# A chain of attention, cross-attention and 32 routed experts: down projection as three products of 12-bit halves, norm weights moved to the gathered rows, splits of 1024 columns

## The chip, the cores and the metric

The kernel runs on one core of one Trainium2 chip. The metric is the device time of one execution in microseconds (us). A core has a matrix engine (TensorE, PE in the profile; its weight loads are PEld), three engines for elementwise work (VectorE or DVE, ScalarE or ACT, GpSimd or POOL), and SyncE (SP), which here issues DMAs. Each engine runs its own instructions strictly in the order in which they stand in its queue; semaphores order them between engines.

## The reference, cut to what matters

A decoder layer on 1024 rows of 1024 columns: attention and retention (not touched here), a cross-attention, then a mixture of 32 experts, of which each row is sent to two.

```python
def rms_norm(x, g):
    y = xf * lax.rsqrt(jnp.mean(xf * xf, axis=-1, keepdims=True) + EPS)
    return (y * g).astype(x.dtype)
...
    x = x + memory_cross_attention(...)                       # "x2" in the kernel
    hm = rms_norm(x, moe_norm_g[l])
    x = x + hierarchical_moe(hm, ...)
...
        a = jnp.einsum('sd,edf->sef', hr, w_gate)             # 1024 -> 256, each expert
        u = jnp.einsum('sd,edf->sef', hr, w_up)
        act = jax.nn.silu(a) * u * gate[:, :, None]
        return jnp.einsum('sef,efd->sd', act, w_down)         # 256 -> 1024
```

All is float32. The kernel computes an expert only for the rows sent to it, in lists of 96 rows (`CAP`).

## The kernel before, in words

Most matrix products are made as three products of halves. A number x is split into H, x rounded to a 12-bit mantissa (type `F32R`, a copy on ACT), and L = x - H (on DVE); then `mm3` (L145) adds up H*H, H*L and L*H in PSUM. `split` (L151) makes the halves; with a `scale` it multiplies on the way (L157 on ACT, L158 on DVE), without one it is L154 and L155.

The last two stages matter here.

- *End of the cross-attention* (763 to 862 us of the profiled execution). For each of eight tiles of 128 rows, `column` (L1077) makes x2 (L1087 adds the residual), sums squares, and when a tile is whole SP writes it to DRAM twice (L1091): to `x2d`, from which the experts gather rows, and to `out`, into which the experts add. Tiles are transposed for the router's logits. Then the reciprocal norm `rx` (a power on POOL, L168) and the lists of rows are made (862 to 881).
- *The experts* (881 to 1226), `moe` (L1478). Expert e's weights come by `load_up` (gate and up, 1 MB each) and `load_down` (1 MB), issued on SP into rings of five raw buffers each; up to five experts are loaded ahead. A list's rows are gathered from `x2d` by POOL's indirect DMA (L1411) into `xg`, transposed by PE and split into xH and xL (`expert_x`, two blocks b0, b1). `expert_up` splits the gate and up weights with the norm's weights `g8` as the scale, one 128x512 slice n at a time, in four pairs j0 to j3 (`half` 0 and 1), and `mm3` adds them up in one PSUM tile `ps_pj`. `expert_act`: silu on ACT (`sl`, L1448), product on DVE (`act`, L1450). `expert_actT`: two PE transposes (L1456), a copy on ACT (`aT`, L1459). `expert_out`: the down product in full f32, straight from the raw weights (L1469, `ps_sc`), scaled by the gate into `y` (one half on ACT, L1473, one on DVE, L1471), and added into `out` by POOL's indirect DMA, the scatter (L1474). Scatters into rows of the same group wait for each other.

The loop makes, for expert e, its act, the first half of the up projection of e+1, the transposed act of e, the gathered rows of e+2, the down projection of e, and the second half of the up projection of e+1. A scheduler then orders each engine's queue by a table of priorities (not changed) and by the free buffers of the tiles: `H` and `L` have HB buffers, the gathered rows NX, `y` YB. The chip runs that order; it doesn't depend on what is late at run time.

## Time and profile before

| | us |
|---|---|
| three runs | 1228.27, 1231.3, 1240.53 (median 1231.3) |
| the profiled execution: time | 1227.24 |
| its span, from the first to the last instruction | 1225.4 |
| PE busy | 1160.0 (95%) |
| DVE busy | 791.2 (65%) |
| ACT busy | 657.4 (54%) |
| POOL busy | 154.8 (13%) |
| mean granted TensorE clock (1 is 2.4 GHz) | 0.986 |

The profile is one execution, seen on each engine. PE's share over the whole is high, but a share over the whole mixes stages; what a change to the experts is worth is read from their stage alone, 881 us to the end, which is 28% of the span. By lines, the splits of the expert weights (L158 on DVE, L157 on ACT) and the products (L145, L1469 on PE) are its largest groups. The page's chain of work that ended last gives PE 64% and DMA 19% of the span.

### The profile page before, as it was taken

How to read it: one execution, taken by the hardware profiler on the slowest of the kernel's cores; microseconds unless marked ns; L12 is line 12 of the kernel's file. 1: busy time of each engine (PE TensorE's matmuls, PEld its weight loads, DVE VectorE, ACT ScalarE, POOL GpSimd, SP SyncE). 2: the span in 40 equal slices, each digit the busy share in tenths (PEclk: the TensorE clock that was granted, in tenths of full speed). 3: DMA queues.
4: the chain of work that ended last, by engine and by line, in shares of the span. 5: the costliest groups of instructions: out<-in, count | busy, mean ns of one | idle time of the engine just before them, and what ended most of it. 6: DMA issues, size and time to landing. Idle time of an engine off the chain costs nothing.

```text
span 1225.4 us, 18474 instructions
## 1 busy us (share of the span) xinstructions
PE 1160.0 (95%) x6309; PEld 907.3 (74%) x6309; DVE 791.2 (65%) x2056; ACT 657.4 (54%) x1540; POOL 154.8 (13%) x151
## 2 busy tenths in 40 slices
PE   7999999998799999989999999999699999999994
PEld 6887878776588778878899998778566666666552
DVE  4756465678777877557744445554677777777571
ACT  8723232456455565557644445332477777777571
POOL 1011010121000000000000000000222222222121
PEclk9999999999999999999999999999799999999997
DMA  7622020204223424266621025975799999999972
GB/s 227 180 65 80 10 76 10 89 23 149 87 73 112 147 78 121 86 221 202 221 71 61 27 62 159 329 273 223 239 347 341 334 337 332 321 312 319 316 271 32
DMA packets 115362, 213.25 MB, mean 174 GB/s; under 512 B 20531, under 2 KB 68659, under 8 KB 107073
## 3 DMA queue, kind: packets, MB, share of 16 engines
q1 hardware_dynamic: 108096, 194.66, 46.8%
q0 software_dynamic: 7168, 17.37, 6.1%
q8 instruction: 51, 0.84, 0.3%
q14 instruction: 47, 0.38, 0.1%
HBM read 179.69 MB, written 40.11 MB: 179 GB/s over the span
## 4 chain that ended last, share of the span: by engine, by line
PE 64%; DMA 19%; DVE 6%; ACT 5%; issue 3%; POOL 1%; SPq 0%; POOLq 0%; DVEq 0%; ACTq 0%
PE ps_pj L145 36%; DMA raw<-in_expert_w_up_dram 5%; DMA raw<-in_expert_w_down_dram 5%; PE ps_fl L145 5%; PE ps_sc L1469 4%; PE ps_sc L145 4%; PE ps_po L145 4%; PE ps_tr L162 3%; DMA raw<-in_expert_w_gate_dram 3%; DMA raw<-in_cross_w_kv_dram 2%; DVE wl L158 1%; PE ps_tr L1422 1%; PE ps_pjp L145 1%; DMA raw<-in_cross_w_q_dram 1%; ACT wh L157 1%
## 5 line engine op out<-in xcount | busy, mean ns | idle before, releaser
L145 PE MATMUL ps_pj<-wh,xT 128*128 128x512 f32 (+1 forms) x640 | 218.1, 401 | 1.9 <-ACT wh L157 1.8
L158 DVE SCALAR_TENSOR_TENSOR L<-raw,g,H 128x512 fp32r<-128x512 f32 x256 | 179.9, 746 | 58.4 <-ACT H L157 57.0
L157 ACT ACTIVATE H<-raw,g 128x512 fp32r<-128x512 f32 x256 | 169.4, 713 | 34.7 <-PE ps_pj L145 22.6
L145 PEld LDWEIGHTS ps_pj<-wh,xT 128*128 128x128 f32 x640 | 120.1, 189 | 21.0 <-ACT wh L157 2.7
L145 PE MATMUL ps_pj<-wl,xT 128*128 128x512 f32 (+1 forms) x320 | 126.3, 395 | 0.0
L1469 PE MATMUL ps_sc<-raw,aT 128*96 128x512 f32 x256 | 117.6, 602 | 1.0 <-ACT aT L1459 1.0
L145 PE MATMUL ps_pj<-H,xH 128*96 128x512 f32 x256 | 116.3, 454 | 0.3 <-ACT H L157 0.3
L145 PE MATMUL ps_pj<-L,xH 128*96 128x512 f32 x256 | 102.8, 401 | 0.6 <-DVE L L158 0.6
L145 PE MATMUL ps_pj<-H,xL 128*96 128x512 f32 x256 | 101.5, 397 | 0.0
L1469 PEld LDWEIGHTS ps_sc<-raw,aT 128*96 128x96 f32 x256 | 39.1, 162 | 64.9 <-issue 51.1
L1474 POOL DMA_INDIRECT out_dram<-y,idx x32 | 59.6, 1863 | 208.8 <-ACT H L157 163.2
L145 PE MATMUL ps_pj<-x1TH,wh 128*128 128x256 f32 x256 | 74.3, 290 | 2.3 <-ACT x1TH L154 2.3
L145 PE MATMUL ps_pj<-x1TL,wh 128*128 128x256 f32 x256 | 75.3, 294 | 0.0
L145 PE MATMUL ps_pj<-x1TH,wl 128*128 128x256 f32 x256 | 74.4, 291 | 0.0
L145 PEld LDWEIGHTS ps_pj<-wl,xT 128*128 128x128 f32 x320 | 60.7, 190 | 8.0
L145 PEld LDWEIGHTS ps_pj<-H,xH 128*96 128x96 f32 x256 | 42.5, 166 | 23.5 <-issue 7.2
L145 PEld LDWEIGHTS ps_pj<-L,xH 128*96 128x96 f32 x256 | 41.6, 163 | 22.9 <-DVE L L158 9.1
L453 ACT ACTIVATE tg<-ps_pj,rh 128x128 f32<-128x128 f32 x32 | 11.7, 365 | 84.9 <-PE ps_pj L145 84.7
L145 PEld LDWEIGHTS ps_pj<-H,xL 128*96 128x96 f32 x256 | 41.4, 162 | 15.4 <-issue 0.3
L145 PEld LDWEIGHTS ps_pj<-x1TH,wh 128*128 128x128 f32 x256 | 48.5, 189 | 2.7 <-ACT x1TH L154 2.7
L1023 ACT ACTIVATE cP<-ps_sc,cnb,fcq 128x256 f32<-128x256 f32 x32 | 17.8, 558 | 58.5 <-DVE cnb L1018 58.5
L145 PEld LDWEIGHTS ps_pj<-x1TH,wl 128*128 128x128 f32 x256 | 48.6, 190 | 0.0
(410 smaller groups left out, 2898.1 us busy)
## 6 DMA issues: line engine op xcount, KB each, us to landing
raw<-in_expert_w_down_dram SPq DMA_DIRECT2D x32, 1024.0 KB
raw<-in_expert_w_gate_dram SPq DMA_DIRECT2D x32, 1024.0 KB
raw<-in_expert_w_up_dram SPq DMA_DIRECT2D x32, 1024.0 KB
raw<-in_w_in_dram SPq DMA_DIRECT2D x32, 256.0 KB
raw<-in_cross_w_kv_dram SPq DMA_DIRECT2D x32, 256.0 KB
x<-x1d SPq DMA_DIRECT2D x16, 512.0 KB
xr<-in_x_dram SPq DMA_DIRECT2D x16, 256.0 KB
raw<-in_w_out_dram SPq DMA_DIRECT2D x16, 256.0 KB
```

What stands on the lines that cost most here:

```text
L145: mm = lambda s, m, i, e: self.nc.tensor.matmul(out, s, m, start=i, stop=e, skip_group_check=skip)
L157: self.high = nc.scalar.activation(H, src, AF.Copy, scale=scale)
L158: return nc.vector.scalar_tensor_tensor(L, src, scale, H.bitcast(F32), OP.mult, OP.subtract)
L162: self.nc.tensor.transpose(dst[:, i * 128:(i + 1) * 128], src[:, i * 128:(i + 1) * 128], self.ident)
L453: nc.scalar.activation(tg, p[:, 384:512], AF.Tanh, scale=rh[:, tb:tb + 1])
L1023: nc.scalar.activation(P[:, js], s[:, js], AF.Exp, bias=nb[:, j:j + 1], scale=f[:, j:j + 1], accum_out=su[:, j:j + 1])
L1422: nc.tensor.transpose(tr[:, k * CAP:(k + 1) * CAP], xg[:CAP, 4 * b + k::8], self.ident[:CAP, :CAP])
L1469: nc.tensor.matmul(py[:CAP], act[:, j * CAP:(j + 1) * CAP], wd[:, j, cs], start=(j == 0), stop=(j == 1))
L1474: return nc.gpsimd.indirect_dma_start(out=self.out, out_offset=bass.IndirectOffsetOnAxis(ap=rows, axis=0), in_=y[:CAP], in_offset=None, co ...
```

## The change

The down projection's weights and the transposed activation are now split, and the product is made by `mm3` (three f32r products for each f32 one). The norm's weights `g8` are no longer multiplied into the expert weights; instead a copy `gx` of the norm's weights on all partitions is multiplied into x2 before it is written to `x2d`: on POOL a whole tile at a time (`gained`), in the last tile in pieces, one on POOL and two on DVE. Splits of the expert weights have 128x1024 elements instead of 128x512 (six per expert on each of ACT and DVE, four for gate and up and two for down, where it was eight), so HB goes from 6 to 4; NX goes from 4 to 3 and YB from 4 to 2. Both halves of `y` are written by ACT. The down weights are laid out as the others are, two neighbouring rows on a partition, and the activation is transposed with a stride of 2 to match. In the diff, the new places are L1095 and L1100 (multiply), L1400 (load), L1436 (transposes of rows), L1455 (`expert_split`), L1462 and L1464 (`sl`, `act`), L1470 (transposes of act) and L1485 (`y`).

```diff
--- before.py
+++ after.py
@@ -50,8 +50,8 @@
 ND = 5
 RING = {"gu": (0, 4, 4, 5), "dn": (1, 1, 5, 5)}
 LOADS = ["u0", "u1", "", "u2", "", "u3", "d1", "d2d3d4"]
-NX = 4
-YB = 4
+NX = 3
+YB = 2
 HP = 1
 XB = 4
 WK = 2
@@ -69,7 +69,7 @@
 ES = 1
 SP = 0
 OB = 2
-HB = 6
+HB = 4
 HALVES = [(slice(0, 64), slice(64, 128)), (slice(64, 128), slice(0, 64))]
 TWO_PI = 2.0 * math.pi
 C1 = 6.28125
@@ -151,7 +151,7 @@
 
         nc = self.nc
         if scale is None:
-            nc.scalar.activation(H, src, AF.Copy)
+            self.high = nc.scalar.activation(H, src, AF.Copy)
             return nc.vector.tensor_tensor(L, src, H.bitcast(F32), OP.subtract)
         else:
             self.high = nc.scalar.activation(H, src, AF.Copy, scale=scale)
@@ -1052,7 +1052,7 @@
         s2 = self.s2
         self.s2l = sm.tile([128, 1], F32, name="s2l", bufs=1)
         self.r2 = sm.tile([128, NT], F32, name="rx2", bufs=1)
-        x2s, ocs, oTs, pls, hs, ps = {}, {}, {}, {}, {}, {}
+        x2s, ocs, oTs, pls, hs, ps, gs = {}, {}, {}, {}, {}, {}, {}
 
         def load_oc(tb):
             if tb < NT:
@@ -1087,8 +1087,18 @@
             nc.vector.tensor_tensor(x2[:, cols], p, x2[:, cols], OP.add)
             self.square(self.s2l if q.start else s2[:, tb, c:c + 1], x2[:, cols], p)
             if cols.stop == D:
-                for dst in (self.x2d, self.out):
-                    nc.sync.dma_start(dst[tb * 128:(tb + 1) * 128, :], x2)
+                nc.sync.dma_start(self.out[tb * 128:(tb + 1) * 128, :], x2)
+            if tb == NT - 1:
+                if q.start == 0:
+                    gs[c] = self.slot([128, 512], name="ocl", bufs=OB, pool=self.OT)
+                g = gs[c][:, q]
+                (nc.vector if c else nc.gpsimd).tensor_tensor(g, x2[:, cols], self.gx[:, cols], OP.mult)
+                nc.sync.dma_start(self.x2d[tb * 128:(tb + 1) * 128, cols], g)
+
+        def gained(tb):
+
+            nc.gpsimd.tensor_tensor(x2s[tb], x2s[tb], self.gx, OP.mult)
+            nc.sync.dma_start(self.x2d[tb * 128:(tb + 1) * 128, :], x2s[tb])
 
         def transposed(tb, i, n=4):
 
@@ -1181,11 +1191,15 @@
                         column(tb, 1, slice(0, 8), slice(0, 256))
                         logits(j, 0)
                         transposed(tb - 1, 1)
+                        gained(tb - 1)
                         column(tb, 1, slice(0, 4), slice(256, 512))
                         transposed(tb, 1, 2)
                     with self.at("fl1", j):
                         logits(j, 1)
                     end(j)
+                    if tb + 1 < NT:
+                        gained(tb - 1)
+                        gained(tb)
                 with self.at("fbeg", tb):
                     begin(tb + 2)
                 load_oc(tb + 3)
@@ -1199,8 +1213,8 @@
 
         nc, a, G = self.nc, self.a, self.G
         one = lambda shape, name, dtype=F32, pool=G: pool.tile(shape, dtype, name=name, bufs=1)
-        self.g8 = one([128, 8], "g8")
-        nc.sync.dma_start(self.g8, a["moe_norm_g"][0].rearrange("(p k) -> p k", k=8))
+        self.gx = one([128, D], "gx", pool=self.P)
+        nc.sync.dma_start(self.gx, a["moe_norm_g"][0].partition_broadcast(128))
         self.wr = one([128, 8, 36], "wr", pool=self.P)
         gm = one([128, 8], "gm", pool=self.P)
         nc.sync.dma_start(gm, a["moe_norm_g"][0].rearrange("(k p) -> p k", p=128))
@@ -1383,7 +1397,7 @@
         w = self.a[("expert_w_gate", "expert_w_up", "expert_w_down")[i]][0]
         w = w[e] if isinstance(e, int) else w[bass.ds(e, 1)].rearrange("o r n -> (o r) n")
         k = 8 if i < 2 else 2
-        self.nc.sync.dma_start(t, w.rearrange("(p k) n -> p k n" if i < 2 else "(k p) n -> p k n", k=k))
+        self.nc.sync.dma_start(t, w.rearrange("(p k) n -> p k n", k=k))
 
     def load_up(self, n, part=slice(0, 2), late=None):
 
@@ -1428,23 +1442,23 @@
     def expert_up(self, p, xT, raw, half, first=False):
 
         for j in (2 * half, 2 * half + 1):
-            ws = []
-            for n in (2 * j, 2 * j + 1):
-                H = self.MW.tile([128, 2, FF], F32R, name="H", tag="H", bufs=HB)
-                L = self.MW.tile([128, 2, FF], F32R, name="L", tag="L", bufs=HB)
-                l = self.split(H, L, raw[:, :, n], self.g8[:, n:n + 1])
-                if first:
-                    self.after(l, self.listed, "rows of the lists first")
-                elif self.aT and half == 0:
-                    self.after(self.high, self.aT, "act of the expert before first")
-                ws.append((H.rearrange("p s n -> p (s n)"), L.rearrange("p s n -> p (s n)")))
-            for n in (2 * j, 2 * j + 1):
-                self.mm3(p, *xT[n], *ws[n % 2], n == 0, n == 7)
+            (H, L), l = self.expert_split(raw[:, :, 2 * j:2 * j + 2])
+            if first:
+                self.after(l, self.listed, "rows of the lists first")
+            elif self.aT and half == 0:
+                self.after(self.high, self.aT, "act of the expert before first")
+            for n in range(2):
+                self.mm3(p, *xT[2 * j + n], H[:, :, n], L[:, :, n], n + j == 0, n + 2 * j == 7)
+
+    def expert_split(self, raw):
+
+        HL = [self.MW.tile(list(raw.shape), F32R, name=x, tag=x, bufs=HB) for x in "HL"]
+        return HL, self.split(*HL, raw)
 
     def expert_act(self, p, r):
 
         nc, M = self.nc, self.M
-        sl = M.tile([128, FF], F32, name="sl", tag="sl", bufs=2)
+        sl = M.tile([128, FF], F32, name="sl", tag="sl", bufs=1)
         nc.scalar.activation(sl[:CAP], p[:, :FF], AF.Silu, scale=r)
         act = M.tile([128, FF], F32, name="act", tag="act", bufs=2)
         nc.vector.scalar_tensor_tensor(act[:CAP], p[:, FF:], r, sl[:CAP], OP.mult, OP.mult)
@@ -1453,24 +1467,22 @@
     def expert_actT(self, act):
         tr = self.bank("tra")
         for j in range(2):
-            self.nc.tensor.transpose(tr[:, j * CAP:(j + 1) * CAP], act[:CAP, j * 128:(j + 1) * 128],
-                                     self.ident[:CAP, :CAP])
-        aT = self.M.tile([128, 2 * CAP], F32, name="aT", tag="aT", bufs=2)
-        self.aT = self.nc.scalar.activation(aT, tr[:, :2 * CAP], AF.Copy)
-        return aT
+            self.nc.tensor.transpose(tr[:, j * CAP:(j + 1) * CAP], act[:CAP, j::2], self.ident[:CAP, :CAP])
+        H, L = [self.M.tile([128, 2 * CAP], F32R, name="a" + x, tag="a" + x, bufs=2) for x in "HL"]
+        self.split(H, L, tr[:, :2 * CAP])
+        self.aT = self.high
+        return [(H[:, j * CAP:(j + 1) * CAP], L[:, j * CAP:(j + 1) * CAP]) for j in range(2)]
 
     def expert_out(self, act, wd, gate, rows):
         nc = self.nc
         y = self.M.tile([128, D], F32, name="y", tag="y", bufs=YB)
         for c in range(2):
             cs = slice(c * 512, (c + 1) * 512)
-            py = self.bank("py")
+            py = self.bank("py")[:CAP]
+            (H, L), _ = self.expert_split(wd[:, :, cs])
             for j in range(2):
-                nc.tensor.matmul(py[:CAP], act[:, j * CAP:(j + 1) * CAP], wd[:, j, cs], start=(j == 0), stop=(j == 1))
-            if c:
-                nc.vector.tensor_scalar(y[:CAP, cs], py[:CAP], gate, None, OP.mult)
-            else:
-                nc.scalar.activation(y[:CAP, cs], py[:CAP], AF.Copy, scale=gate)
+                self.mm3(py, *act[j], H[:, j], L[:, j], j == 0, j == 1)
+            nc.scalar.activation(y[:CAP, cs], py, AF.Copy, scale=gate)
         return nc.gpsimd.indirect_dma_start(out=self.out, out_offset=bass.IndirectOffsetOnAxis(ap=rows, axis=0),
                                             in_=y[:CAP], in_offset=None, compute_op=OP.add, bounds_check=S - 1,
                                             oob_is_err=False)
```

Three places of the queues that the chip is given. First ACT, one expert in the middle of the loop, before. `aT` is the copy of expert n's transposed activation, the `H` rows on `raw_10337` are the eight splits of the gate and up weights of expert n+2, `sl` is expert n+1's silu, `xH` the halves of gathered rows; what stands in brackets is what the instruction waits for.

```order
L1459 ACTIVATE aT_10684<-ps_trb_10681 128x192 [waits PE_49]
L157 ACTIVATE H_10757<-raw_10337,g8_8989 128x512 [waits DMAHW6_49,DMAHW5_49,DVE_49]
L157 ACTIVATE H_10761<-raw_10337,g8_8989 128x512 [waits DVE_49]
L157 ACTIVATE H_10771<-raw_10337,g8_8989 128x512 [waits DVE_49]
L157 ACTIVATE H_10775<-raw_10337,g8_8989 128x512 [waits DVE_49]
L1473 ACTIVATE y_10707<-ps_sc_10708,gate_10128 96x512 [waits DMASW7_49,PE_49]
L157 ACTIVATE H_10825<-raw_10337,g8_8989 128x512 [waits DVE_49]
L157 ACTIVATE H_10829<-raw_10337,g8_8989 128x512 [waits DVE_49,PE_49]
L1448 ACTIVATE sl_10749<-ps_pj_10652,gate_10128 96x256
L157 ACTIVATE H_10839<-raw_10337,g8_8989 128x512 [waits DVE_49,PE_49]
L157 ACTIVATE H_10843<-raw_10337,g8_8989 128x512 [waits DVE_49,PE_49]
```

And after, from one `aH` (what `aT` was) to the next. `raw_10229` are the gate and up weights of expert n+2 (four splits: j0, j1, j2, j3 in this order), `raw_10039` the down weights of expert n+1.

```order
L154 ACTIVATE aH_10574<-ps_trb_10571 128x192 [waits PE_49]
L154 ACTIVATE H_10657<-raw_10229 128x1024 [waits DMAHW5_49,DMAHW6_49,DVE_49,Activation_49]
L154 ACTIVATE xH_10689<-ps_tr_10684 128x384 [waits PE_49]
L1485 ACTIVATE y_10599<-ps_sc_10600,gate_10140 96x512 [waits DMASW1_49,PE_49]
L154 ACTIVATE H_10667<-raw_10229 128x1024
L1485 ACTIVATE y_10599<-ps_sc_10612,gate_10140 96x512 [waits PE_49]
L154 ACTIVATE H_10707<-raw_10039 128x1024 [waits DMAHW2_49]
L154 ACTIVATE H_10719<-raw_10039 128x1024 [waits DVE_49,PE_49]
L154 ACTIVATE H_10735<-raw_10229 128x1024 [waits DVE_49,PE_49]
L154 ACTIVATE xH_10698<-ps_tr_10693 128x384 [waits PE_49]
L154 ACTIVATE H_10745<-raw_10229 128x1024 [waits DVE_49,PE_49]
L1462 ACTIVATE sl_10649<-ps_pj_10550,gate_10140 96x256
```

Before, four splits followed the copy at once, and one `y` stood behind them. Now both `y` rows stand on ACT between the first splits, and the down weights' two splits stand ahead of the third and fourth of gate and up, behind which `sl` waits.

The second place is DVE in the loop, before: one period. `act_10647` belongs to expert n, the `L` rows on `raw_10233` to n+1.

```order
L155 TENSOR_TENSOR xL_10588<-ps_tr_10582,xH_10587 128x384 [waits Activation_49]
L155 TENSOR_TENSOR xL_10597<-ps_tr_10591,xH_10596 128x384 [waits Activation_49]
L158 SCALAR_TENSOR_TENSOR L_10654<-raw_10233,g8_8989,H_10653 128x512 [waits DMAHW4_49,DMAHW3_49,Activation_49]
L158 SCALAR_TENSOR_TENSOR L_10658<-raw_10233,g8_8989,H_10657 128x512 [waits Activation_49]
L158 SCALAR_TENSOR_TENSOR L_10668<-raw_10233,g8_8989,H_10667 128x512 [waits PE_49,Activation_49]
L158 SCALAR_TENSOR_TENSOR L_10672<-raw_10233,g8_8989,H_10671 128x512 [waits PE_49,Activation_49]
L1471 TENSOR_SCALAR y_10603<-ps_sc_10608,gate_10128 96x512 [waits PE_49]
L158 SCALAR_TENSOR_TENSOR L_10722<-raw_10233,g8_8989,H_10721 128x512 [waits Activation_49]
L158 SCALAR_TENSOR_TENSOR L_10726<-raw_10233,g8_8989,H_10725 128x512 [waits Activation_49]
L1450 SCALAR_TENSOR_TENSOR act_10647<-ps_pj_10548,gate_10128,sl_10645 96x256 [waits PE_49,Activation_49]
L158 SCALAR_TENSOR_TENSOR L_10736<-raw_10233,g8_8989,H_10735 128x512 [waits Activation_49]
L158 SCALAR_TENSOR_TENSOR L_10740<-raw_10233,g8_8989,H_10739 128x512 [waits Activation_49]
```

And after, from `aL`, the low half of expert n's activation, to `act` of expert n+1; `raw_10229` and `raw_10039` are as for ACT.

```order
L155 TENSOR_TENSOR aL_10575<-ps_trb_10571,aH_10574 128x192 [waits Activation_49]
L155 TENSOR_TENSOR L_10658<-raw_10229,H_10657 128x1024 [waits DMAHW6_49,DMAHW5_49,Activation_49]
L155 TENSOR_TENSOR xL_10690<-ps_tr_10684,xH_10689 128x384 [waits PE_49,Activation_49]
L155 TENSOR_TENSOR L_10668<-raw_10229,H_10667 128x1024 [waits DVE_49,Activation_49]
L155 TENSOR_TENSOR L_10708<-raw_10039,H_10707 128x1024 [waits DMAHW2_49,Activation_49]
L155 TENSOR_TENSOR L_10720<-raw_10039,H_10719 128x1024 [waits Activation_49]
L155 TENSOR_TENSOR xL_10699<-ps_tr_10693,xH_10698 128x384 [waits PE_49,Activation_49]
L155 TENSOR_TENSOR L_10736<-raw_10229,H_10735 128x1024 [waits DVE_49]
L155 TENSOR_TENSOR L_10746<-raw_10229,H_10745 128x1024 [waits Activation_49]
L1464 SCALAR_TENSOR_TENSOR act_10651<-ps_pj_10550,gate_10140,sl_10649 96x256 [waits Activation_49]
```

`act` stood between two pairs of `L` rows; now it stands behind all `L` rows of the up projection, and one `xL` row stands between the down weights' `L` rows and those of j2 and j3.

The third place is PE after, behind the first product of j2 (`H_10735`) and up to the transposes of expert n+1's activation (`ps_trb`). `ps_tr` are transposes of gathered rows, `H_10745` is j3. Before, the same two transposes stood apart, each between products.

```order
L1436 MATMUL ps_tr_10799<-ident_89,xg1_10097 128x96 [waits DVE_49]
L1436 MATMUL ps_tr_10799<-ident_89,xg1_10097 128x96 x3
L145 MATMUL ps_pj_10656<-L_10736,xH_10592 96x512 [waits DVE_49]
L145 MATMUL ps_pj_10656<-H_10735,xL_10593 96x512
L145 MATMUL ps_pj_10656<-H_10735,xH_10592 96x512
L145 MATMUL ps_pj_10656<-L_10736,xH_10592 96x512
L145 MATMUL ps_pj_10656<-H_10735,xL_10593 96x512
L145 MATMUL ps_pj_10656<-H_10745,xH_10592 96x512 [waits Activation_49]
L145 MATMUL ps_pj_10656<-L_10746,xH_10592 96x512 [waits DVE_49]
L145 MATMUL ps_pj_10656<-H_10745,xL_10593 96x512
L1470 MATMUL ps_trb_10677<-ident_89,act_10651 128x96 [waits DVE_49,PE_49]
L1470 MATMUL ps_trb_10677<-ident_89,act_10651 128x96
```

The activation's transposes, for which ACT's `aH_10680` waits, stand behind all products of j2 and half of those of j3.

## Rows read from the trace of the kernel before

**Rows 1.** Window of the whole core: busy us of each engine (instructions), clock, DMA share, GB/s.

```profile
900.00:950.00 50.00, 50.00 (x204) 29.77 (x203) 37.67 (x60) 35.32 (x64) 14.08 (x10) 1.00 1.00 342
```

**Rows 2.** The chain of work that ended last: start, us, what; experts 0 and 11.

```profile
891.75 3.62 PE ps_sc L1469 x8
...
1004.07 3.65 PE ps_sc L1469 x8
```

**Rows 3.** The same chain, first and last load of weights.

```profile
865.90 4.54 DMA raw<-in_expert_w_gate_dram
...
1131.84 29.94 DMA raw<-in_expert_w_up_dram
```

**Rows 4.** Timelines of ACT and POOL at the end: start, us, what.

```profile
1200.31 0.31 ACT L1459 ACTIVATE aT<-ps_trb 128x192 f32<-128x192 f32 x1
...
1212.72 1.40 POOL L1474 DMA_INDIRECT out_dram<-y,idx  x1 [5.42 <-DMA out_dram<-y,idx]
```

**Rows 5.** Timelines of PE, then of ACT, within one expert.

```profile
961.28 0.39 PE L145 MATMUL ps_pj<-H,xL 128*96 128x512 f32 x1
961.51 0.39 PE L145 MATMUL ps_pj<-H,xH 128*96 128x512 f32 x1
...
962.53 0.25 PE L1456 MATMUL ps_trb<-ident,act 96*128 96x96 f32 x1
...
962.81 0.33 ACT L1459 ACTIVATE aT<-ps_trb 128x192 f32<-128x192 f32 x1 [1.30 <-PE ps_trb L1456]
```

**Rows 6.** Groups by line, 840 to 1160: count, busy us, mean ns, idle before.

```profile
L158 DVE SCALAR_TENSOR_TENSOR L<-raw,g,H 128x512 fp32r<-128x512 f32 x224 | 158.0, 747 | 48.8 <-ACT H L157 47.4 <-issue 0.3
L157 ACT ACTIVATE H<-raw,g 128x512 fp32r<-128x512 f32 x224 | 148.4, 713 | 30.8 <-PE ps_pj L145 22.6 <-DMA raw<-in_expert_w_up_dram 5.3 <-DMA out_dram<-x 2.9
...
L155 DVE TENSOR_TENSOR xL<-ps_tr,xH 128x384 fp32r<-128x384 f32 x58 | 29.8, 552 | 13.0 <-ACT xH L154 13.0
...
L154 ACT ACTIVATE xH<-ps_tr 128x384 fp32r<-128x384 f32 x58 | 27.0, 490 | 26.3 <-PE ps_tr L1422 26.1
...
L1473 ACT ACTIVATE y<-ps_sc,gate 96x512 f32<-96x512 f32 x26 | 17.4, 671 | 0.2 <-PE ps_sc L1469 0.2
...
L1450 DVE SCALAR_TENSOR_TENSOR act<-ps_pj,gate,sl 96x256 f32<-96x256 f32 x27 | 12.8, 474 | 0.7 <-ACT sl L1448 0.7
L1448 ACT ACTIVATE sl<-ps_pj,gate 96x256 f32<-96x256 f32 x27 | 12.2, 453 | 0.0
L1459 ACT ACTIVATE aT<-ps_trb 128x192 f32<-128x192 f32 x27 | 8.9, 330 | 33.0 <-PE ps_trb L1456 33.0
```

**Rows 7.** Timelines of ACT, then of DVE: two and four splits in a row.

```profile
958.37 1.33 ACT L157 ACTIVATE H<-raw,g 128x512 fp32r<-128x512 f32 x2
...
953.57 2.74 DVE L158 SCALAR_TENSOR_TENSOR L<-raw,g,H 128x512 fp32r<-128x512 f32 x4 [1.67 <-ACT H L157]
```

**Rows 8.** Lines L154 and L155, whole span: ns min/median/max, first and last start.

```profile
L154 ACT ACTIVATE wh<-raw x8: 1048/1061/1068, 408.2 to 755.0; 128x1024 fp32r<-128x1024 f32 x8
...
L155 DVE TENSOR_TENSOR wl<-raw,wh x8: 1217/1226/1226, 409.3 to 756.1; 128x1024 fp32r<-128x1024 f32 x8
```

**Rows 9.** Timeline of ACT at the start of the experts.

```profile
891.32 0.33 ACT L1459 ACTIVATE aT<-ps_trb 128x192 f32<-128x192 f32 x1 [0.97 <-PE ps_trb L1456]
```

**Rows 10.** End of the cross-attention: the chain on PE, and POOL's timeline.

```profile
857.34 0.44 PE ps_tr L162 x4
...
862.43 0.69 POOL L168 TENSOR_TENSOR rx<-v_rx,mhalf 128x2 f32<-128x2 f32 x1 [27.61 <-DVE v_rx L1142]
```

**Rows 11.** Window near the end of the loads.

```profile
1196.00:1198.00 2.00, 2.00 (x10) 1.40 (x9) 2.00 (x4) 0.49 (x1) 2.00 (x1) 1.00 0.01 4
```

**Rows 12.** Windows of four us with PE half idle, and what followed one.

```profile
540.00:544.00 4.00, 1.66 (x11) 0.99 (x9) 2.36 (x6) 2.81 (x6) 0.00 (x0) 1.00 0.94 308
590.00:594.00 4.00, 2.19 (x10) 1.43 (x8) 3.22 (x5) 3.26 (x7) 0.00 (x0) 1.00 0.82 276
594.00:598.00 4.00, 3.56 (x18) 3.43 (x19) 3.20 (x6) 2.61 (x5) 0.00 (x0) 0.57 0.28 59
```

## The prediction

> **What bounds the kernel now.** I read the windows by stage first, then the chain of work that ended last, then the groups by line, and last the timelines of a single expert. From 891 to 1200 us the kernel does its 32 experts, and there TensorE (PE) has no gap: it is busy 50.00 of 50 us from 900 to 950, as in the four windows of 50 us after that, beside 37.67 on DVE, 35.32 on ACT and a DMA share of 1.00 [rows 1]. The chain there is PE work alone; the full f32 products of the down projection begin at 891.75 for expert 0 and at 1004.07 eleven experts later, so 10.21 us for each [rows 2]. After that the chain runs back through loads of weights, up to an up projection that lands at 1161.78 [rows 3]: the weights come a little slower than PE eats them, and the lead of five preloaded experts is used up. Then PE leads again until ACT copies the activation of expert 30 at 1200.31; the last scatter is issued at 1212.72, after the one before it has landed, and 12.7 us later all is over [rows 4]. So two limits lie close together, PE at 10.21 us per expert and the stream of weights; DVE has 12 us of rest in 50, ACT 15.
>
> **PE gets lighter.** The eight f32 pieces of an expert's down projection take 3.65 us in the chain [rows 2]. Twelve f32r products take their place. Issues of such products stand 0.23 us apart (961.28, 961.51) [rows 5], so twelve are 2.76 us. PE's work per expert falls from 10.21 to 10.21 - 3.65 + 2.76 = 9.3 us.
>
> **ACT and DVE get heavier.** Before, an expert has on ACT eight splits of 713 ns, two of 490, sl 453, aT 330 and y 671 [rows 6]. Neighbours overlap: two splits of 713 take 1.33 us together and four of 747 on DVE take 2.74 [rows 6, 7], so 0.095 and 0.083 us come off each in a row. After, a split has 1024 columns: 1061 ns on ACT, 1226 on DVE, in the same form for other weights of this kernel [rows 8]. There are six per expert (four for gate and up, two for down) and both halves of y are on ACT. In a row ACT needs 6 x 0.966 + 2 x 0.395 + 2 x 0.576 + 0.358 + 0.235 = 8.3 us (7.1 before), DVE 6 x 1.143 + 2 x 0.469 + 0.391 + about 0.3 (aL, which is new; by ACT's 128x192 and DVE's 128x384 it lies between 0.33 and 0.55) = 8.5. Both are still under 9.3, so a count of work says: faster. The queues say something else.
>
> **The new loop, read from the order.** Call aH(n), the copy of expert n's transposed activation, time zero. ACT's queue then holds, in this order, H(j0) of expert n+2, xH, y0, H(j1), y1, both halves of the down weights of n+1, H(j2), xH, H(j3), sl of n+1, aH(n+1). DVE's has xL, L(j2), L(j3) and only then act of n+1; PE's has all of j2 and half of j3 ahead of the two transposes that aH(n+1) waits for. Before, act stood between the two pairs of L, and y's second half was on DVE. Engines run their queues in order, so this is a ring, and I add it up:
> - aH, H(j0), xH: 0.235 + 0.966 + 0.395 = 1.6. y0 waits for six down products: aH ends at 0.33, 6 x 0.23 for the issues, and 0.16 that a product's record (0.39 us) goes on after the next issue [rows 5], so 1.95 to 2.0.
> - y0, H(j1), y1, two down splits: 2 x 0.576 + 3 x 0.966 = 4.05. H(j2) starts at 6.05.
> - H(j2) 0.966, xH 0.490: 7.51. DVE's xL 0.469: 8.0. L(j2) runs to 9.23, L(j3) to 10.37, act to 10.76.
> - PE has from 9.26 on L(j2)'s first product, four more of j2, one of j3, two of L(j3)'s round: 8 x 0.23 = 1.84, so 11.1. The two transposes, 0.09 apart and 0.25 long, end at 11.44, and the copy starts 0.03 later (962.78 to 962.81 before [rows 5]).
>
> The ring closes at 11.47 us, say **11.5 us per expert against 10.21**. In it ACT rests 2.7 us (for sl is done at 8.7) and PE 2.2. The weights don't bind in it: from the fifth expert's gate at 865.90 to the up of the 29th at 1161.78 [rows 3] they came every 11.8 us, so the ring eats 0.3 us of the lead per expert, 9 in all, of a lead of some 47 (four experts). Bounds of the period: 11.2 if the hand-overs cost nothing, 11.8 if each of six costs 0.05 more.
>
> **Sum.** Before, aT(0) is at 891.32 [rows 9]. The lists, the gathers and PE's work of expert 0 set it, and all stay; I keep it. The first round has seven ACT splits rather than six and two xH late in it: 13.5 (bounds 11.5 and 15). Then 29 x 11.5 = 333.5: aH(30) at 1238.3. From aT(30) to the end it is 25.1 us now (1200.31 to 1225.4 [rows 4]): the products get 0.9 shorter, the two y follow one another (0.6 longer), the wait of the last scatter stays. Span 1263.4, plus 1.84 between span (1225.4) and time (1227.24) of the profiled execution: **1265**. That execution lies 4 us under the median of 1231.3 and 1 us under the lowest run shown, so the step to be seen against the median is +34 us, 2.8%.
>
> **Edits costed at nothing.** The multiply by the norm's weights moves from the splits to the rows of x2, on POOL. Tile 6 is free after its transposes at 857.78, and POOL's next work is rx at 862.43 [rows 10], so 4.6 us are free. No POOL elementwise of that size is in the trace; below it DVE's 1226 ns bounds it. Above 4.6, every us goes straight into the lists and all after them. The Trainium skill, "GPSIMD Engine Reference" (the side-by-side table of measured times), has 4497 ns for twice as many columns; by it an estimate is 2.3 us and the sum stays. The last tile's second half, on DVE, adds a 256-column multiply at the very end, less than the 0.55 that 384 columns take [rows 6]; the gathers wait for the lists, which come later than x2d, and if that cover is gone it is +0.5. The 512 KB of gx are 1.5 us of DMA at the 342 GB/s of [rows 1], in a stage that PE leads, as the chain has it at 857.34 [rows 10]: +1.5 without that cover. Smaller lists of buffers (NX 3, YB 2, HB 4): y is rewritten two experts later, 23 us, against a scatter that lands within the 12.7 of the end [rows 4]; HB 4 lets H(j2) wait for j0's products, done by 4.9 in the count above against 6.05.
>
> **Rivals.**
> 1. *PE sets the pace after all* (faster). The ring would have to close under PE's 9.3, as the counts of work say. Then the weights bind: they are all in by 1196, as the DMA share of 0.01 after that shows [rows 11]. Two splits, products, y of the last expert need some 5 us: last scatter 1201, span 1213.7, **1215**. Against it: the queue orders above. It decides at a ring of 10.2 us: (1200.3 - 891.3 - 12.5) / 29.
> 2. *No change.* If hand-overs hide one split's worth (the ring at 10.2 to 10.6), gain and loss cancel: 891.3 + 12.5 + 29 x 10.4 + 25.1 + 1.8 = **1232**. For it: DVE could be ahead of what I take at xL.
> 3. *The clock falls in the ring* (much slower). In the ring PE has one product and four transposes (0.66 us) in the 2.6 us ahead of L(j2). A stretch with 2.19 busy of 4 us was followed by a granted clock of 0.57, but one with 1.66 kept 1.00 [rows 12]. At half clock, 1.2 GHz, the 1.84 + 0.3 us of PE work ahead of aH nearly double: a ring of 13.4, **1320** if in every period. The Trainium skill, "TensorE: Matmul & The Clock Gate" (A second HAM failure mode), tells of a kernel whose clock swung because PE idled briefly between groups of matmuls; by it this rival would be the likeliest, by the row at 1.00 it needn't happen.
>
> **How the numbers follow.** My forecast 0.66: 1252 to 1278 (29 x 0.3 either way, first round and tail 2 each, in part cancelling). Rival 1: 0.14. Rival 2: 0.12. Rival 3: 0.08, part of it below 1290. The range 1222 to 1290 leaves out rival 1 and most of rival 3. 1% is about what a measurement of this kernel can tell from no change: faster 0.14, same 0.12, slower 0.74.
>
> **What would show it.** In the stage of the experts: aH to aH 11.5 us apart; PE busy about 81%, clock 1.00; ACT idle 2.7 us ahead of each aH, released by PE's transposes, and L(j2) waiting behind xL; DMA share high until all weights are in near 1196, then next to nothing for 40 us while the experts go on; no ACT wait for raw at the end. Wrong if aH stands 10 us apart or less, if the clock is under 0.95, or if rx on POOL moves past 863.

## The result, and the profile after

The kernel became slower, by more than the prediction's range allowed.

| | before | after |
|---|---|---|
| median, us | 1229.87 (4 runs beside after's) | 1305.59 (1298.63 to 1306.3) |
| ratio on record, 95% interval (the two medians give 1.0616) | 1 | 1.0589 (1.0561 to 1.0617) |
| span of the profiled execution | 1225.4 | 1303.2 |
| PE / DVE / ACT / POOL busy | 1160.0 / 791.2 / 657.4 / 154.8 | 1192.4 / 827.7 / 696.6 / 183.0 |
| mean granted clock | 0.986 | 0.959 |

Four marks cut the two spans: the first `cnb` on DVE in the cross-attention (L1018, a softmax bias of 128x2, which a recorded expectation calls the first split; ahead of everything the change touches; some lines later in kernels with added lines), `rx` on POOL, the first and the 31st copy of a transposed activation (aT or aH).

| stretch, us | before | predicted | after |
|---|---|---|---|
| start to L1018 | 609.17 | 609.17 | 620.71 |
| L1018 to rx | 253.26 | 253.26 | 254.44 |
| rx to aH(0) | 28.89 | 28.89 | 30.92 |
| aH(0) to aH(30) | 308.99 | 347.0 | 373.60 |
| aH(30) to the end | 25.1 | 25.1 | 23.5 |

The rows of after: timelines (start, us, what; in brackets the idle time before and who ended it). First aH(0) and aH(30), which end the third and the fourth stretch:

```profile
906.07 0.33 ACT L154 ACTIVATE aH<-ps_trb 128x192 fp32r<-128x192 f32 x1
...
1279.67 0.31 ACT L154 ACTIVATE aH<-ps_trb 128x192 fp32r<-128x192 f32 x1
```

Then one round of ACT in the middle of the experts:

```profile
1008.15 0.33 ACT L154 ACTIVATE aH<-ps_trb 128x192 fp32r<-128x192 f32 x1 [2.92 <-PE ps_trb L1470]
1008.37 1.05 ACT L154 ACTIVATE H<-raw 128x1024 fp32r<-128x1024 f32 x1
1009.33 0.48 ACT L154 ACTIVATE xH<-ps_tr 128x384 fp32r<-128x384 f32 x1
1010.18 0.69 ACT L1485 ACTIVATE y<-ps_sc,gate 96x512 f32<-96x512 f32 x1 [0.38 <-PE ps_sc L145]
...
1012.29 2.95 ACT L154 ACTIVATE H<-raw 128x1024 fp32r<-128x1024 f32 x3
1015.13 0.48 ACT L154 ACTIVATE xH<-ps_tr 128x384 fp32r<-128x384 f32 x1
1015.50 1.06 ACT L154 ACTIVATE H<-raw 128x1024 fp32r<-128x1024 f32 x1
1016.45 0.47 ACT L1462 ACTIVATE sl<-ps_pj,gate 96x256 f32<-96x256 f32 x1
1019.83 0.33 ACT L154 ACTIVATE aH<-ps_trb 128x192 fp32r<-128x192 f32 x1 [2.91 <-PE ps_trb L1470]
```

In the same round DVE, then PE:

```profile
1013.49 2.35 DVE L155 TENSOR_TENSOR L<-raw,H 128x1024 fp32r<-128x1024 f32 x2
1015.76 0.55 DVE L155 TENSOR_TENSOR xL<-ps_tr,xH 128x384 fp32r<-128x384 f32 x1
1016.23 2.35 DVE L155 TENSOR_TENSOR L<-raw,H 128x1024 fp32r<-128x1024 f32 x2
1018.50 0.47 DVE L1464 SCALAR_TENSOR_TENSOR act<-ps_pj,gate,sl 96x256 f32<-96x256 f32 x1
```

```profile
1015.29 0.47 PE L145 MATMUL ps_pj<-H,xH 128*96 128x512 f32 x1 [0.25 <-ACT H L154]
1016.36 0.68 PE L1436 MATMUL ps_tr<-ident,xg 96*128 96x96 f32 x4 [0.61 <-DVE xL L155]
1017.50 0.47 PE L145 MATMUL ps_pj<-L,xH 128*96 128x512 f32 x1 [0.45 <-DVE L L155]
1017.80 0.39 PE L145 MATMUL ps_pj<-H,xL 128*96 128x512 f32 x1
...
1019.43 0.36 PE L1470 MATMUL ps_trb<-ident,act 96*128 96x96 f32 x2
```

This is the ring of the prediction, instruction by instruction: ACT has nothing left after sl and waits 2.9 us for PE's transposes; these stand on PE behind eight products, the first of which waits 0.45 us for L(j2); and L(j2) stands on DVE behind xL. PE does not wait for act itself: act is done at 1018.97 (1018.50 + 0.47), and the transposes follow the products at 1019.43 without a gap. A round at full clock is 11.68 us (1008.15 to 1019.83). The waits of ACT over the stage (us in total, times, longest) are those 29 and little else; no wait for weights stands among them:

```profile
ACT aH L154 <- PE ps_trb L1470: 101.6, 29, 4.4
ACT y L1485 <- PE ps_sc L145: 15.9, 30, 2.2
ACT H L154 <- PE ps_pj L145: 2.1, 2, 1.8
```

But not every round is at full clock. Windows (busy us of PE, PEld, DVE, ACT, POOL with counts; granted clock, DMA share, GB/s):

```profile
1000.00:1050.00 50.00, 44.78 (x187) 29.49 (x186) 34.86 (x41) 33.93 (x50) 12.73 (x8) 0.93 0.95 306
...
1064.00:1068.00 4.00, 2.70 (x12) 1.50 (x11) 4.00 (x5) 2.56 (x4) 1.50 (x2) 1.00 0.85 263
1068.00:1072.00 4.00, 4.00 (x19) 2.64 (x18) 2.19 (x4) 2.13 (x4) 0.00 (x0) 1.00 1.02 324
...
1100.00:1104.00 4.00, 2.67 (x12) 1.53 (x12) 4.00 (x5) 3.18 (x5) 1.56 (x2) 1.00 0.57 116
1104.00:1108.00 4.00, 4.00 (x12) 2.43 (x11) 1.80 (x5) 0.75 (x2) 0.55 (x1) 0.57 0.76 246
```

After the gap of some rounds the clock falls to a mean of 0.57 for 4 us, that is most of the time at the lower level of 1.2 GHz, just where PE's products stand ahead of the transposes; after others it stays at 1.00. PE's busy time in the stretch before (2.67 against 2.70) does not tell the two apart. The 30 rounds go 14.6, 13.1, 12.7, 12.0, 13.2, 13.0, 11.7, 11.7, 11.7, 13.2, 12.9, 11.8, 11.7, 11.7, 13.2 and so on: of the 29 behind the first, 17 are longer than 11.8, up to 13.4.

### The profile page after: what moved, and what is told of

The parts are those of the page before. It is cut to its first block, busy times and chain, and to the rows that moved or that the text cites. A ratio compares the mean times of both kernels' runs of the same rounds, so it can differ in the third digit from the quotient of the medians.

```text
span 1303.2 us, 18690 instructions
## 1 busy us (share of the span) xinstructions
PE 1192.4 (91%) x6437; PEld 952.5 (73%) x6437; DVE 827.7 (64%) x1994; ACT 696.6 (53%) x1508; POOL 183.0 (14%) x159
## 4 chain that ended last, share of the span: by engine, by line
PE 62%; DVE 17%; DMA 7%; ACT 6%; issue 5%; POOL 1%; SPq 1%; DVEq 0%; POOLq 0%; ACTq 0%
PE ps_pj L145 33%; PE ps_sc L145 11%; DVE L L155 9%; PE ps_fl L145 5%; PE ps_po L145 4%; PE ps_tr L162 3%; DMA raw<-in_cross_w_kv_dram 1%; DVE wl L158 1%; DVE xL L155 1%; PE ps_pjp L145 1%; DMA raw<-in_cross_w_q_dram 1%; ACT wh L157 1%; DMA x1d<-xo 1%; PE ps_sc L475 1%; PE ps_trp L162 1%
## 5 line engine op out<-in xcount | busy, mean ns | idle before, releaser
L155 DVE TENSOR_TENSOR L<-raw,H 128x1024 fp32r<-128x1024 f32 x192 | 226.5, 1217 | 25.7 <-ACT H L154 25.4
L154 ACT ACTIVATE H<-raw 128x1024 fp32r<-128x1024 f32 x192 | 195.1, 1050 | 4.3 <-PE ps_pj L145 4.3
L145 PE MATMUL ps_pj<-L,xH 128*96 128x512 f32 x256 | 113.4, 443 | 16.4 <-DVE L L155 16.4
L145 PE MATMUL ps_pj<-H,xL 128*96 128x512 f32 x256 | 108.3, 423 | 0.0
L1486 POOL DMA_INDIRECT out_dram<-y,idx x32 | 66.7, 2086 | 229.6 <-ACT y L1485 213.8
L154 ACT ACTIVATE aH<-ps_trb 128x192 fp32r<-128x192 f32 x32 | 10.6, 330 | 101.6 <-PE ps_trb L1470 101.6
L1436 PEld LDWEIGHTS ps_tr<-ident,xg 96*128 96x128 f32 x256 | 36.3, 200 | 37.8 <-DVE xL L155 25.0
L1436 PE MATMUL ps_tr<-ident,xg 96*128 96x96 f32 x256 | 40.7, 284 | 24.8 <-DVE xL L155 15.9
L155 DVE TENSOR_TENSOR xL<-ps_tr,xH 128x384 fp32r<-128x384 f32 x64 | 35.2, 553 | 38.5 <-ACT H L154 33.7
L453 ACT ACTIVATE tg<-ps_pj,rh 128x128 f32<-128x128 f32 x32 | 11.7, 366 | 84.8 <-PE ps_pj L145 84.6
L145 PE MATMUL ps_sc<-H,aH 128*96 128x512 f32 x128 | 53.1, 415 | 2.4 <-ACT aH L154 2.4
```

The costliest lines, as they stand in the source:

```text
L145: mm = lambda s, m, i, e: self.nc.tensor.matmul(out, s, m, start=i, stop=e, skip_group_check=skip)
L154: self.high = nc.scalar.activation(H, src, AF.Copy)
L155: return nc.vector.tensor_tensor(L, src, H.bitcast(F32), OP.subtract)
L453: nc.scalar.activation(tg, p[:, 384:512], AF.Tanh, scale=rh[:, tb:tb + 1])
L1436: nc.tensor.transpose(tr[:, k * CAP:(k + 1) * CAP], xg[:CAP, 4 * b + k::8], self.ident[:CAP, :CAP])
L1486: return nc.gpsimd.indirect_dma_start(out=self.out, out_offset=bass.IndirectOffsetOnAxis(ap=rows, axis=0), in_=y[:CAP], in_offset=None, co ...
```

## The experiments

The total mixes the change with where L1018 falls, which differs by up to 12 us between the programs below (last experiments). So beside each ratio stands the time from aH(0) to aH(30), "T": 309.0 before, 373.6 after. In second profiles of the same two kernels (last experiments) T is 311.0 and 376.7, so a difference of 3 us in T says nothing.

**Does the clock fall because PE rests?** After, with five products per expert added in PE's gap, into an idle PSUM bank that nobody reads.

```diff
+FILL = 5
...
+                    d = mm(p, xH, h, False, False)
+                    spare = self.bank("po")[:CAP]
+                    for k in range(FILL):
+                        e = mm(spare, xH, h, True, True)
+                        self.after(e, d, "work for the gap")
...
```

> The changed kernel with five extra f32r products per expert, written to a spare bank that nobody reads, queued on PE behind the first product of j2, where PE waits for xL and then for L(j2). Nothing else moves. Theory (the clock falls because PE rests there): clock 1.00 in the whole expert stage, every round 11.7 us instead of a mix of 11.7 and 13.2, aH(30) some 20 us earlier, time about 1285. Rival (the clock falls for another reason, or the long rounds have another cause): the mix of rounds stays, time 1300 to 1306.

Ratio 1.0371 (1.033 to 1.0413), 1276.64 us: 29 us less than after, by adding work. T is 353.3, 20.3 less than after's 373.6; from the third round to the 28th all are 11.7 but one. ACT's wait is that of a fast round, 84.8 / 29 = 2.9 us, and the clock holds:

```profile
ACT aH L155 <- PE ps_trb L1484: 84.8, 29, 3.2
```

```profile
1020.00:1070.00 50.00, 48.38 (x219) 33.15 (x218) 36.67 (x43) 36.34 (x53) 16.12 (x9) 1.00 0.96 317
```

So the falls of the clock cost the experts 20 us, and PE's rest is what brings them. Most of the rest of the total lies ahead of aH(0) (899.5 against 906.1), which the expected 1285 did not count on.

**Does the order make the ring?** After, with two numbers of the priority table changed, so that sl, act and its transposes come ahead of the splits and products they stood behind. The order changes on ACT, DVE and PE at once, so the run doesn't tell which of the three moves counts.

```diff
-PRI = {..., 'ma': -200, ...}
+PRI = {'mu1': 50, ..., 'ma': 0, ...}
```

> The changed kernel with two numbers of the priority table changed, so that sl and act of the next expert stand right behind H(j0) and L(j0) and no longer behind the splits of j2 and j3. Same instructions, same work. Theory (the ring through act, not the amount of work, sets 11.7 us): rounds of 9.4 to 9.8 us by PE's work until the weights bind, then 11 to 12 by the stream of weights; all weights in near 1208, time 1225 to 1240. Rival (ACT and DVE have too much work after the change): rounds stay above 11, time above 1280.

Ratio 1.0037 (1.0007 to 1.0066), 1235.5 us: 70 us off after, with the same work; 65.3 of them are in T (308.3 against 373.6). Rounds are 9.8 us, nearly the 9.3 that the prediction counted for PE, until the nineteenth. Then they are 11.3, 11.2, 11.8, 10.5, 13.2: ACT waits for weights.

```profile
ACT H L154 <- DMA raw<-in_expert_w_up_dram: 17.7, 6, 4.3
```

```profile
1020.00:1070.00 50.00, 49.44 (x236) 36.18 (x236) 44.92 (x54) 43.89 (x64) 18.86 (x11) 1.00 0.97 323
1070.00:1120.00 50.00, 47.16 (x215) 32.73 (x214) 39.56 (x48) 37.73 (x56) 16.45 (x9) 1.00 0.98 326
```

T is no better than before's 309.0: the kernel outruns the weights and waits for them.

**Is it the weights that take the gain back?** The last kernel without the down weights' loads after the fifth expert's (it reuses older ones).

```diff
-        down = lambda e: self.load_down(e) if e < NE else None
+        down = lambda e: self.wd.append(self.wd[e - ND]) if e < NE else None
```

> The kernel of e2_order without the loads of down weights after the fifth: later experts take the old weights from the ring (wrong data, a third of the expert weights' traffic gone). Queues are otherwise the same. Theory (in e2_order the stream of weights took back what PE won, from the 20th expert on): rounds of 9.8 us to the end, aH(30) 294 us after aH(0) and not 308, time about 1221 to 1225. Rival (the long rounds late in e2_order come from the queues): rounds of 10 to 13 us late as there, time 1235.

Ratio 0.9919 (0.9891 to 0.9947), 1220.52 us. T is 293.9, 9.8 in every round but the first (10.0) and the last (9.1); the DMA engines are no longer full:

```profile
1070.00:1120.00 50.00, 49.54 (x240) 36.43 (x239) 44.72 (x52) 43.83 (x61) 18.57 (x11) 1.00 0.87 270
```

The stream of weights therefore costs the re-ordered kernel 14.4 us (308.3 - 293.9).

**And after itself?** The same leaving out of loads in the changed kernel.

> The changed kernel without the loads of down weights after the fifth, as in e5. Theory (the changed kernel's ring doesn't wait for weights): the same rounds of 11.7 and 13.2 us, time 1298 to 1306. Rival (transfers slow the engines' reads or hold the ring): rounds shorter than 11.4, time under 1290.

Ratio 1.0582 (1.0532 to 1.0632), T 372.0, rounds still of 11.7 to 13.3, at a DMA share of 0.65. The weights do not bind in the ring.

**One part alone.** First, after with the transposed activation and the down product back in f32, unsplit, so with the moved norm, the splits of 1024, both halves of y on ACT and the smaller lists of buffers:

```diff
...
-            (H, L), _ = self.expert_split(wd[:, :, cs])
-                self.mm3(py, *act[j], H[:, j], L[:, j], j == 0, j == 1)
+                nc.tensor.matmul(py, act[:, j * CAP:(j + 1) * CAP], wd[:, j, cs], start=(j == 0), stop=(j == 1))
```

> The changed kernel with the down projection left as a full f32 product from the raw weights, so without the down weights' two splits; splits of 1024, the norm's weights in the rows, both y on ACT and the smaller buffer lists stay. Theory (the two down splits make the ring longer than PE's work): rounds of 10.2 us by PE, clock 1.00, time near 1239 if the stage before takes as long as in the changed kernel, near 1227 if as before. Rival (splits of 1024 with four buffers make the ring): rounds above 11, time above 1270.

Ratio 0.9999 (0.9977 to 1.0021), T 304.2, rounds 10.1, PE busy 50.00 of 50 at clock 1.00. Then before with the norm's move alone (L1095, L1100; `split` without its scale):

> The kernel before with only the norm's weights moved into the rows; splits of 512, full f32 down projection, buffer lists as before. Theory (the multiply costs 1 to 2 us at the end of the cross-attention and nothing in the experts; the 11.5 us that the profile of the changed kernel lost before 768 us are not its doing): 1229 to 1234. Rival (the multiply on POOL or the load of gx delays the start of the experts by 12 to 15 us): 1242 to 1246.

Ratio 1.0014 (0.9988 to 1.004), T 307.9. Then before with the down projection's split alone, in pieces of 512 (y's buffers three instead of four; the transposed activation is split as in after):

```diff
...
-                nc.tensor.matmul(py[:CAP], act[:, j * CAP:(j + 1) * CAP], wd[:, j, cs], start=(j == 0), stop=(j == 1))
+                H, L = [self.MW.tile([128, 512], F32R, name=x, tag=x, bufs=HB) for x in "HL"]
+                self.split(H, L, wd[:, j, cs])
+                self.mm3(py[:CAP], *act[j], H, L, j == 0, j == 1)
```

> The kernel before with the down projection alone as three products of halves: its weights split in four pieces of 512 columns per expert (YB 3 for room), the norm's weights and the other splits as before, one half of y on DVE. By rows, DVE then has 10.0 us of work per expert, ACT 8.9, PE 9.3. Theory (a queue order that puts work of three engines in one ring costs more than any engine's work): rounds of 11 to 12 us with PE resting, time 1255 to 1290. Rival (the busiest engine sets the pace): rounds of 10.0 to 10.3, time 1225 to 1235. If theory holds, splits of 1024 are not what made the ring.

Ratio 1.0628 (1.0574 to 1.0682), 1310.95 us, T 386.4, most rounds of 12.4 to 13.2, longer than the theory's 11 to 12, clock 0.93, no engine full:

```profile
1020.00:1070.00 50.00, 42.58 (x180) 29.20 (x179) 39.90 (x67) 35.96 (x67) 18.17 (x8) 0.93 0.88 285
```

So the loss comes with the split of the down projection under this table of priorities, and with neither of the other parts. The moved norm costs nothing that the total can show. The splits of 1024 columns are not needed for the loss: T is larger without them (386.4 against 373.6), but the two kernels differ in the norm, y and the buffers too, and the clock falls in both, so that these splits make it smaller is not shown.

**More lead for the weights?** Two attempts to make the re-ordered kernel beat before. First, of the raw buffers six for gate and up and three for down, instead of five and five, and the places of the first loads to match.

```diff
-NGU = 5
-ND = 5
...
+NGU = 6
+ND = 3
...
```

> The kernel of e2_order with the same room for raw weights shared out otherwise: six buffers for gate and up, three for down (it was five and five), so that gate and up, which an expert needs two rounds before its down weights, come earlier and the last three transfers are down weights. Theory (the stream of weights binds late in e2_order and its last gate and up come too late): the rounds after the 20th a little shorter at the end, aH(30) 2 to 6 us earlier after aH(0) than the 308 us there, time 1229 to 1234. Rival (the stream binds whatever comes first): 1235 as in e2_order.

Ratio 1.01 (1.0072 to 1.0128): worse. The wait moved to the other ring, from the thirteenth round on:

```profile
ACT H L154 <- DMA raw<-in_expert_w_down_dram: 15.7, 13, 3.1
```

The same buffers in before:

> The kernel before with that same sharing of buffers (six and three). Theory: with PE at 10.2 us per expert the weights hardly bind (5.3 us of waits), so at most 3 us are to be had: 1227 to 1231. Rival (three buffers for down weights are too few): waits for down weights, 1235 or more.

Ratio 1.0119 (1.0084 to 1.0153), with PE waiting for the same weights, so three down buffers are too few for either kernel:

```profile
PE ps_sc L1472 <- DMA raw<-in_expert_w_down_dram: 7.2, 4, 2.9
```

Second, the up weights of the fifth expert not held back for the first gathers.

```diff
-        self.load_up(NGU - 1, slice(1, 2), g)
+        self.load_up(NGU - 1, slice(1, 2))
```

> The kernel with the ring broken (act ahead of the down splits of the priorities), with one edit: the up weights of the fifth expert are no longer held back until the first rows are gathered, so they and the loads behind them on SP's queue start as soon as their buffers are there. In the run with the ring broken the DMA engines moved next to nothing from 880 to 886 us (share 0.09, 0.00, 0.50), while that hold lasted. Theory (from the nineteenth expert on the stream of weights sets the pace; its lead is all that counts): 4 to 6 us of stream are 1.3 to 2 MB more lead, so the rounds of 11 us and more begin later or are fewer, and the time is 4 to 6 us under 1235.5: 1229 to 1232. Rival (the hold is there for a reason: the gathers of the first rows share the DMA engines with 1 MB of weights): the first aH comes 2 to 4 us later than 902.9 and the time stays at 1235 or above.

Ratio 1.009 (1.0065 to 1.0114): the rival. From rx (870.99) to aH(0) (907.35) it is 36.4 us, against 31.4 with the hold; in it PE waits 12.1 us for gathered rows, against 8.6. And no lead is won: T is 308.1 against 308.3, and the slow rounds begin at the same one. The buffers are full sooner and then the queue waits; the DMA share from 900 to 910 is 0.32 where it was 0.88:

```profile
900.00:910.00 10.00, 9.22 (x46) 6.62 (x45) 8.33 (x11) 8.53 (x11) 1.76 (x1) 1.00 0.32 104
```

No version here that loads all its weights beats before. That the five buffers bound the lead fits these rows; more buffers of both kinds were not tried.

**Why does L1018 come 11.5 us later, ahead of all changed work?** Both kernels again, unedited.

> The changed kernel once more, unedited. What it did to the stages before 768 us is none of its doing if theory (their clock falls by chance of the execution, as 609 to 621 us for the first instruction of line L1018 in the profiles so far suggests) holds: that instruction lands anywhere from 609 to 621, and the time moves with it, 1293 to 1306. Rival (the change itself shifts those stages): 620 to 621 again and 1305.

> The kernel before, unedited, for a second profile of it. Theory (when the cross-attention's first split comes, line 1018, varies by execution with the clock granted in the stages ahead of it): somewhere from 609 to 617 us, not 609.17 again within a microsecond; the clock from 285 to 450 us then differs from 0.99. Rival (it hangs on the program: this one has 609, the changed one 621): 608.5 to 610, clock 0.99 again. The experts' rounds are 10.2 us either way, and the time 1230.

After again: 1303.5 us, ratio 1.0579 (1.053 to 1.0628), L1018 at 620.55 (first time 620.71). Before again: 1233.22 us, ratio 0.9999 (0.9976 to 1.0021), L1018 at 608.99 (609.17). Both came back within 0.2 us, against the theory that it drifts by chance. That the program alone decides is not shown by this: there are two profiles of each, both of before are among its fastest executions (1227.24 and 1228.34 us, clock 0.986), and others of before, without a profile, took up to 1241.35 at a clock of 0.976. The trace shows where the two programs part. PE in the retention stage, before and then the kernel with the moved norm alone:

```profile
288.70 0.50 PE L145 MATMUL ps_pj<-wh,oTL 128*128 128x512 f32 x1 [0.54 <-DVE oTL L155]
289.04 0.40 PE L145 MATMUL ps_pj<-wh,oTH 128*128 128x512 f32 x1
289.27 0.39 PE L145 MATMUL ps_pj<-wl,oTH 128*128 128x512 f32 x1
289.50 0.39 PE L145 MATMUL ps_pj<-wh,oTL 128*128 128x512 f32 x1
```

```profile
288.69 0.50 PE L145 MATMUL ps_pj<-wh,oTL 128*128 128x512 f32 x1 [0.54 <-DVE oTL L155]
289.03 0.57 PE L145 MATMUL ps_pj<-wh,oTH 128*128 128x512 f32 x1
289.39 0.63 PE L145 MATMUL ps_pj<-wl,oTH 128*128 128x512 f32 x1
289.82 0.63 PE L145 MATMUL ps_pj<-wh,oTL 128*128 128x512 f32 x1
```

The same products start within 0.01 us of each other, and then issue 0.23 apart in one and 0.43 in the other: the clock has fallen in one only. After shows the same fall at the same products (289.60 to 290.03) and more of them later, a granted clock of 0.92 from 285 to 450 us where before has 0.99. Why it falls there in one profile and not in another stays open. The edit need not lie there: the kernel with five dummy products, which differs from after in the experts alone, has L1018 at 613.74. The others have it at 609.49 (down in f32), 613.67 (norm alone), 614.11 and 614.47 (buffers), 616.03 (after without loads), 616.31, 616.55 and 616.92 (three of the re-ordered), 618.14 (down alone).

## Why the prediction was wrong

The sign was right and so was the ring, but 40 us are missing, half of them by a mechanism to which the prediction gave a chance of 0.08: predicted span 1263.4, measured 1303.2. Two of the three signs that the prediction named for being wrong came: the clock is 0.93 from 1000 to 1050 us, and rx on POOL is at 875.15, past 863 even without the 11.54 us by which L1018 came later. By its own steps:

- **The ring** (right; 11.47 predicted, 11.68 measured). Every station stands where it was read from the order. The 0.2 us are half xL, half PE: xL was put at 7.51 after aH, right behind xH, but DVE is still on an L of the down weights (1013.49 and 2.35 more), so it starts at 7.61; and from L(j2)'s first product to the transposes it is 1.93 us (1017.50 to 1019.43), not 8 x 0.23 = 1.84, for the first product takes 0.30 to the next issue. The bound of 11.8 held. Over 29 rounds, from the 11.5 used, 29 x 0.18 = 5.2 us. First round 14.6 instead of 13.5 (inside its bound of 15): 1.1.
- **The clock in the ring** (wrong; the step that failed). The prediction gave rival 3 a chance of 0.08, and its forecast a clock of 1.00, on the row with 1.66 us busy that kept it [rows 12]. That row showed only that the clock need not fall; the other row of the same group showed that it can. Neither carried a chance near 0 over 30 rounds of the same pattern. Measured: 373.6 - 14.6 - 29 x 11.68 = 20.3 us, and 20.3 by the dummy products as well. That these two agree to a tenth is luck: the second profile of after, with a T of 376.7, would give 23. A slow round at its longest is what rival 3 gave for it (13.4 there and here); but the result is a mixture, for which the text had no case: it had the ring at 11.5 always or at 13.4 always. The Trainium skill, "TensorE: Matmul & The Clock Gate" (A second HAM failure mode), by which the prediction had rival 3 as the likeliest, tells of a clock that swings between its two levels when PE idles briefly between groups of matmuls; the trace agrees, with a clock of 0.93 in the window after and 1.00 with the gap filled.
- **aH(0) kept at 891.32** (wrong by 14.75: 11.54 + 1.18 + 2.03 in the table above). The largest part lies in stages that the diff does not touch, and no row of before told it; only the spread of its runs, 1228 to 1240, hinted at it. The last 2 us go with the gathers: the first takes POOL 4.01 us, before 1.61, and PE waits 8.8 us for the rows, before 5.4 (part of which other waits hide). Why it takes longer stays open.

```profile
870.73 2.40 POOL L1100 TENSOR_TENSOR x<-x,gx 128x1024 f32<-128x1024 f32 x1 [3.34 <-ACT ps_pj L342]
875.15 0.69 POOL L168 TENSOR_TENSOR rx<-v_rx,mhalf 128x2 f32<-128x2 f32 x1 [2.02 <-DVE v_rx L1152]
883.78 4.01 POOL L1425 DMA_INDIRECT xg<-x2d,src  x1 [7.94 <-DVE lg L1318]
```

- **The multiply on POOL costs nothing** (right for the multiply ahead of rx, not for the whole move of the norm). It takes 2.40 us, and rx waits for DVE, not for it (2.02 us idle before rx). The estimate by the Trainium skill, "GPSIMD Engine Reference" (Elementwise — side-by-side cycle accounting), was 2.3 us, and the trace agrees. But from L1018 to rx it is 253.2 to 253.6 us in the four profiles of kernels without the move and 254.3 to 257.5 in the ten with it (254.3 to 256.1 in the eight whose clock stayed at 1.00 there): some 1 to 3 us, too little for the total to show (ratio 1.0014 with that part alone). They come between 771 and 806 us of before's time, where `gx` is loaded and the first tiles are multiplied. The prediction had +1.5 for that load if PE did not cover it. In after DVE waits there for the router's weights, issued on SP behind `gx`, where before it did not; that this is the whole reason is not shown.

```profile
771.41 0.45 DVE L1209 TENSOR_TENSOR wr<-wr,gm 128x288 f32<-128x288 f32 x1
...
784.17 0.46 DVE L1223 TENSOR_TENSOR wr<-wr,gm 128x288 f32<-128x288 f32 x1 [1.16 <-DMA wr<-in_router_w_expert_dram]
```

- **Weights don't bind in the ring** (right): T 372.0 without a third of the loads. They were not all in near 1196, though: the DMA share is 0.86 from 1220 to 1230 and 0.18 in the 10 us behind.
- **Tail** 25.1 kept, 23.5 measured (-1.6): the last scatter is issued 10.9 us after aH(30) (1279.67 to 1290.57), before 12.4 [rows 4].
- **Rival 1, the weights behind a faster PE** (not the case, but its mechanism is real): once the order is mended PE goes at 9.8 a round, against the 9.3 counted, and the stream ends it. The rival's 1215 took it that the weights would be in by 1196 as before; the re-ordered kernel has aH(30) at 1211.3.

Sum of the misses: 14.75 + 5.2 + 1.1 + 20.3 - 1.6 = 39.8. It is the whole of it because the 20.3 were taken as what T has left over; what supports them is the run with the dummy products.

## What to carry to other kernels

Counting work by engine says which engine could bind; only the order of the queues says what does: here every engine had less than a round of work, and two numbers of a priority table were worth 70 us while the lighter arithmetic was worth nothing as long as the weights had to be loaded for it. When a change leaves PE with a regular gap, take a mixture of both clock levels as a case of its own, since a row that kept the clock after a similar gap is no evidence over many rounds; dummy products in the gap test it in one run. And compare kernels from a mark inside the changed stage, not by totals alone: stages that nobody edited moved by up to 12 us.

## What the hardware did that was not expected

Five extra products per expert took 20 us off the experts by keeping the granted clock at 1.00. With the same products on PE starting within 0.01 us of each other, the clock at 289 us fell in one profile and not in the other; what comes of it, the place of L1018, came back in second profiles (before 609.17 and 608.99, after 620.71 and 620.55). Loading weights earlier, beside the first gathers, made the first aH come 5 us later behind rx and gave no lead.
